# Pre-added weight blocks in DRAM: started later, of two blocks instead of three, and one more sevenfold pair in two blocks of the up-projection

## The chip, the cores and the metric

The kernel runs on one core of one Trainium2 chip. The metric is the device time of one execution in microseconds (us). The engines named here are TensorE (PE; PEld is its loading of the stationary operand), VectorE (DVE), ScalarE (ACT), GpSimd (POOL) and SyncE (SP). SP, ACT and POOL each have a queue from which they issue DMAs, in order; an instruction that waits holds up what stands behind it in its queue.

## The reference

One layer of a decoder, for 256 tokens and a width of 2048, in float32:

```
u = RMSNorm(h)
proj = u @ w_in                       # 2048 x 16896
A = HGRN2 recurrence (16 heads), B = dilated attention (3 groups of 4 heads, rotary)
h = h + (sigmoid(ga) * (A @ w_proj_a) + sigmoid(gb) * (B @ w_proj_b)) @ w_out
v = RMSNorm(h)
hup = v @ w_up                        # 2048 x 11264
a, b = causal depthwise conv (width 3) of hup, halves of 5632
h = h + (gelu(a) * b) @ w_down        # 5632 x 2048
out = RMSNorm(h)
```

## The kernel before, in words

**Weights as a stream.** All weights come as 300 units of 16 tiles of 128 x 128 (1 MB each), in the order in which TensorE uses them: units 0 to 131 are w_in, 132 to 151 the two projections of the branches, 152 to 167 w_out, and from 168 on w_up and w_down by turns. Each float32 weight is split into two parts, a rounded one (ACT, L368 or L315) and the rest (DVE, L369 or L316), and each product is made of three matmuls. `begin_unit(u)` splits units u to u + 2 and starts the load of u + 3; it also advances the side work (rotary, attention, recurrence, convolution), which stands in `side` as generators. The raw weights have three buffers, so a load waits until DVE is done with an older unit.

**Who sets the order.** The program is written for one thread; a planner then orders the instructions on each engine by their place in the program and by its own estimate of when each one's inputs and buffers are ready. `in_turn` ties a single instruction behind another. What is emitted late can therefore stand earlier on an engine, and the other way round.

**Attention at the start.** Units 0 to 35 give the queries, keys and values of the three attention groups. For each group, `rope_side` needs the halves of `aqraw` and `akraw` swapped; POOL issues two DMAs for it (L632, L633), into `xs_q` and `xs_k`, and DVE goes on at L638. POOL also issues the loads of the two masks (L676, L677) and of the level masks of the recurrence (`lev`, L737). ACT turns `lev` into `cu` (L741). `attention_side` then makes the scores, the softmax (L704, L708), transposes of the probabilities (`tr`, L715) and the output.

**The up-projection.** w_up is taken in 11 blocks of 2 x 512 columns (the a and the b half), with 8 pairs of 128 rows each. A pair is a product of two 2 x 2 block matrices. In mode "P" it is made of eight block products, in mode "S" of seven, with sums of blocks of weights and of inputs (`operands` makes the latter). A block product is three matmuls. The results go to seven sums in PSUM banks (`sevenfold`; `late_bank`), which `unfold` turns into the four wanted blocks: v = p6 - p1 comes first (L598), then ACT makes c21 and c12 from v (L603, L604), and DVE adds p7 (L605), p2 (L607), p5 (L608 and L609), p4 (L610) and p3 (L611). Blocks 0 to 2 have three "S" pairs each, blocks 3 to 10 five, together 49. `up_order` gives the order of the pairs.

**Additions in DRAM.** For each "S" pair one of the needed sums of weight blocks is made in DRAM, ahead of time: SP copies a block from DRAM to DRAM (L255), and POOL issues accumulating DMAs onto it (L256, L257), each of which waits until the one before it has landed. The load of the unit then brings three blocks of raw weights and this sum (L287, L288). `split_s` makes the other sums on DVE (L339, L340, L342). `begin_unit` spreads the additions evenly over `ADD_SPAN` units from unit `ADD_FROM` on.

**Down-projection.** Behind each block from 1 on come parts of the down-projection (`dn`), each in two banks, one for each half of the tokens; blocks 1 and 2 have two units, later blocks four, the last one more. ACT copies the result out (L1066) and POOL adds it to h by an accumulating DMA (L1067).

Of the kernel before, what the change touches and what calls it, by code (L numbers as in the profile page):

```python
# [11 lines left out]
F32 = mybir.dt.float32  # L12
# [3 lines left out]
ALU = mybir.AluOpType  # L16
AX = mybir.AxisListType

P = 128
T = 256  # L20
D = 2048
KD = D // P
# [9 lines left out]
FB = 4  # L32
# [6 lines left out]
UP_PAIRS = "SSPSSPSP"  # L39
# [11 lines left out]

def up_modes(b):

    return "PPPSSPSP" if b < 3 else UP_PAIRS


BOTH = (0, 1)
# [2 lines left out]
def up_order(b):  # L60


    return {0: (0, 1, 2, 5, 3, 7, 4, 6), 1: (0, 1, 2, 3, 5, 4, 6, 7), 2: (0, 1, 2, 3, 5, 4, 6, 7)}.get(b, tuple(range(KD // 2)))

# [63 lines left out]
NUNITS = len(stream_spec()[0]) // UNIT  # L130
MODES = stream_spec()[1]
ADDS = sum(mode == "S" for mode in MODES.values())
ADD_FROM, ADD_SPAN = 20, 140

# [49 lines left out]
def hybrid_block(ctx, tc, x_p, x_t, weights, g1, gf, params, c_rope, c_mask0, c_mask1, c_level, out):  # L186
    nc = tc.nc
    vec, act, pe = nc.vector, nc.scalar, nc.tensor
# [16 lines left out]
    def stage(name):  # L205
        return late["stage"].tile([P, 512], F32, tag="o2", name=name, bufs=6 if "pool" in late else STAGES - 2)
# [4 lines left out]
    def e4(shape, name):  # L211
        return sbe.tile([P] + list(shape), F32, tag="e4", name=name, bufs=4)
# [4 lines left out]
    def bank(i, name):  # L217
        return ps8.tile([P, 512], F32, tag=f"b{i}", name=name)

    def main_bank(name):  # L220
        turn[0] += 1
        return bank((turn[0] - 1) % 4, name)
# [20 lines left out]
    raws, splits, late = {}, {}, {}  # L243
    dram = ctx.enter_context(tc.tile_pool(name="dram", bufs=1, space=bass.MemoryType.DRAM))
    loaded, ready, to_add = [], {}, deque(sorted(u for u, mode in MODES.items() if mode == "S"))

    def add_blocks():

        if not to_add:
            return  # L250
        u = to_add.popleft()
        ready[u] = q = dram.tile([P, 512], F32, tag=f"q2_{u}", name=f"q2_{u}")
        b = [weights[u, :, i * 512 : (i + 1) * 512] for i in range(4)]
        with in_turn(loaded[-1]):
            nc.sync.dma_start(q, b[3])  # L255
        nc.gpsimd.dma_start(q, b[0], accum_op=ALU.add)  # L256
        nc.gpsimd.dma_start(q, b[2], accum_op=ALU.add)  # L257

    ring = [0]
    last = [None, None]  # L260
# [1 line left out]
    @contextmanager  # L262
    def in_turn(*instructions):

        with ExitStack() as stack:
            for i in instructions:
                stack.enter_context(tc.issue_after(i.ins))
            yield
# [44 lines left out]
    def two_parts(hi, lo, src):  # L313

        act.activation(hi, src, AF.Copy)  # L315
        vec.tensor_tensor(lo, src, hi.bitcast(F32), op=ALU.subtract)  # L316

    def pair_tile(name):

        more = late.get("pool")  # L320
        n = ring[0] % (6 if more else 4)
        ring[0] = (n + 1) if more else (n + 1) % 4
        pool, bufs = (wp, 4) if n < 4 else (more, 2)
        return pool.tile([P, 2, 1024], F32R, tag="pair", name=name, bufs=bufs)

    def split_s(u):

        r = raws[u].rearrange("p (b n) -> p b n", b=4)
        pool = late["pool"]

        def parts(name, src):
            t = pair_tile(name)
            hi, lo = t[:, 0].rearrange("p (b n) -> p b n", b=2), t[:, 1].rearrange("p (b n) -> p b n", b=2)
            two_parts(hi, lo, src)
            return [(hi[:, i], lo[:, i]) for i in range(2)]

        b11, b21 = parts(f"sa{u}", r[:, 0:2])
        b22, q2 = parts(f"se{u}", r[:, 2:4])
        vec.tensor_tensor(r[:, 0], r[:, 3], r[:, 0], op=ALU.subtract)  # L339
        vec.tensor_tensor(r[:, 1], r[:, 3], r[:, 1], op=ALU.add)  # L340
        q3, q4 = parts(f"sf{u}", r[:, 0:2])
        vec.tensor_tensor(r[:, 3], r[:, 3], r[:, 2], op=ALU.subtract)  # L342
        g = pool.tile([P, 2, 512], F32R, tag="sg", name=f"sg{u}", bufs=1)
        two_parts(g[:, 0], g[:, 1], r[:, 3])
        splits[u] = {"11": b11, "21": b21, "22": b22, "q3": q3, "q2": q2, "q4": q4, "q1": (g[:, 0], g[:, 1])}

    def split(u):
        if u >= NUNITS or u in splits:
# [36 lines left out]
    def pump(us):  # L385
        debt[0] += us
        while side and debt[0] > 0:
            try:
                debt[0] -= next(side[0])
            except StopIteration:  # L390
                side.popleft()
        if not side:
            debt[0] = min(debt[0], 0.0)

    def drain():
        while side:
            for _ in side[0]:
                pass
            side.popleft()
        debt[0] = 0.0  # L400

    def begin_unit(u):
        for v in range(u, u + LOOKAHEAD + 1):
            split(v)
        load(u + LOOKAHEAD + 1)
        pump(SIDE_US)
        if u >= ADD_FROM and (u - ADD_FROM) * ADDS // ADD_SPAN < ADDS:
            while len(to_add) > ADDS - 1 - (u - ADD_FROM) * ADDS // ADD_SPAN:
                add_blocks()
# [110 lines left out]
    def moving_step(pst, parts, k, k0, nk):  # L520

        hi, lo = next_tiles(4)
        for m in range(2):
            xh, xl = parts(k, m)
            pe.matmul(pst[m], xl, hi, start=(k == k0), stop=False)  # L525
            pe.matmul(pst[m], xh, hi, start=False, stop=False)  # L526
            pe.matmul(pst[m], xh, lo, start=False, stop=(k == k0 + nk - 1))  # L527

    def moving(parts, k0, nk, name, pst=None):

        pst = pst or [main_bank(f"{name}_{m}") for m in range(2)]
        for k in range(k0, k0 + nk):
            moving_step(pst, parts, k, k0, nk)
        return pst
# [2 lines left out]


    PRODUCTS = {
        "S": ((1, "a11", "11"), (2, "a12", "21"), (6, "x2", "q2"), (3, "x4", "22"), (7, "x3", "q3"), (4, "a22", "q4"), (5, "x1", "q1")),  # L540
        "P": (
            (2, "a11", "11"), (2, "a12", "21"), (4, "a21", "11"), (4, "a22", "21"),
            (5, "a21", "12"), (5, "a22", "22"), (3, "d1", "12"), (3, "d2", "22"),
# [32 lines left out]
    def sevenfold(ops, modes_of, order, name):  # L576

        sums = {i: late_bank(i, f"{name}_{i}") for i in range(1, 8)}
        left = {i: sum(p[0] == i for mode in modes_of for p in PRODUCTS[mode]) for i in sums}
        fresh = set(sums)  # L580
        for i in order:
            w = next_pair()
            for b, x, n in PRODUCTS[modes_of[i]]:
                (xh, xl), (wh, wl) = ops[i][x], w[n]
                left[b] -= 1
                pe.matmul(sums[b], xl, wh, start=b in fresh, stop=False)  # L586
                pe.matmul(sums[b], xh, wh, start=False, stop=False)  # L587
                pe.matmul(sums[b], xh, wl, start=False, stop=left[b] == 0)  # L588
                fresh.discard(b)
        return sums  # L590
# [269 lines left out]
    def four(name, by_half=False):  # L860

        t = e4([2, HG, P], name) if name[0] == "q" else w4([2, HG, P] if by_half else [HG, T], name)
        for h in range(HG):
            ps = stationary(x_pair, KD, f"{name}p{h}")
            if by_half:
                second = w1(f"{name}t{h}")
                act.activation(second, ps[:, T:], AF.Copy)
                vec.tensor_tensor(t[:, :, h], halves(ps[:, :T]), halves(second), op=ALU.add)
            else:
                summed(ps, t[:, h], f"{name}t{h}")  # L870
        if by_half:
            r = halves(rstd)[:, :, None, :].to_broadcast([P, 2, HG, P])
        else:
            r = rstd[:, None, :].to_broadcast([P, HG, T])
        vec.tensor_tensor(t, t, r, op=ALU.mult)
        return t
# [6 lines left out]
    for g in range(NGRP):  # L883
        z = four(f"z{g}", True)
        f = e4([2, HG, P], f"f{g}")
        act.activation(f, z, AF.Sigmoid)
        act.activation(z, z, AF.Sigmoid, scale=-1.0)
        for h in range(HG):
            i = g * HG + h
            vec.tensor_scalar(f[:, :, h], f[:, :, h], lb[:, 1, i : i + 1], lb[:, 0, i : i + 1], op0=ALU.mult, op1=ALU.add)  # L890
            vec.tensor_scalar(z[:, :, h], z[:, :, h], lb[:, 1, i : i + 1], None, op0=ALU.mult)
        q = four(f"q{g}", True)
# [4 lines left out]
        pst = moving(x_parts, 0, KD, f"gp{g}")  # L897
# [79 lines left out]
    for j in range(NJ):  # L977
        pst = moving(mix_parts, 0, KD, f"wo{j}")
# [23 lines left out]
    def late_bank(i, name):  # L1002
        return bank(place[i], name)
# [50 lines left out]
    for b in range(NBLK):  # L1054
        sums = sevenfold(hv, up_modes(b), up_order(b), f"up{b}")
        drain()
        side.append(hidden_side(b, sums))
        pump(0.0001)
        for j, b0, b1 in DOWN.get(b, ()):
            pst = moving(ff_parts, b0 * FB, (b1 - b0) * FB, f"dn{b}_{j}", [late_bank(i, f"dn{b}_{j}_{i}") for i in ((4, 5) if j % 2 else (1, 6))])  # L1060
            for m in range(2):
                if b == NBLK - 1:
                    vec.tensor_tensor(ht[j][:, m], ht[j][:, m], pst[m], op=ALU.add)
                else:
                    t = stage(f"dns{b}_{j}_{m}")
                    act.activation(t, pst[m], AF.Copy)  # L1066
                    nc.gpsimd.dma_start(ht[j][:, m], t, accum_op=ALU.add)  # L1067
# [9 lines left out]
    for m in range(2):  # L1077
# [16 lines left out]
        v, r, t = v3[:, mc], r3[:, mc], s3[:, mc]  # L1094
# [57 lines left out]
```

## Time and profile before

| | |
|---|---|
| median of three runs | 1750.25 us (1747.96 to 1752.4) |
| profiled execution | 1752.61 us, its span 1750.8 us |
| mean granted TensorE clock | 0.994 |
| ACT busy | 1035.4 us (59%) |
| POOL busy | 120.5 us (7%) |
| accumulates of POOL onto a sum (L256, L257) | 98, of 256 KB, median 6.4 us to landing |
| copies of SP (L255) | 49, of 256 KB, median 5.6 us |

How to read the lines of the profile that follow: times are us from the start of the span. A row of a timeline has start, duration, engine, line of the kernel, operation, and output <- inputs by tile names without their numbers; in brackets stands the idle time of that engine before it and what ended it. A row of the waits has the engine and what it did next, what it waited for, the sum, the number of times and the longest. A row of a table of stretches has the stretch, its length, the busy time of PE, PEld, DVE, ACT and POOL with the number of instructions, the granted clock of TensorE (1.00 is full), the busy share of the 16 DMA engines and GB/s. Matmuls overlap, so the distance of two starts, not the duration, is what one costs.

### The profile page before, as it was taken

Reading aid. Unit: us, or ns where it says so; the run is one execution under the profiler, and the core shown is the slowest. Engines: PE = TensorE matmul, PEld = TensorE weight load, DVE = VectorE, ACT = ScalarE, POOL = GpSimd, SP = SyncE. Lnnn points to the kernel's source line nnn. Section 1 sums busy time; section 2 is a strip of 40 time slices with the busy share of each in tenths; the row PEclk is TensorE's granted clock in tenths of the full one; section 3 lists DMA queues with packets and bytes.
Section 4 is the critical chain, followed back from the end, with each engine's and each line's share of the span. In section 5 each row is a group of like instructions: output and inputs, shape, how many; then the busy total and the mean of one; then the engine's idle time right before and its main releaser. Section 6 shows DMA issues by size and latency. Waiting matters only on the chain.

```text
span 1750.8 us, 21856 instructions
## 1 busy us (share of the span) xinstructions
PE 1720.1 (98%) x8325; PEld 1441.0 (82%) x8325; DVE 1299.6 (74%) x1562; ACT 1035.4 (59%) x1414; POOL 120.5 (7%) x159
## 2 busy tenths in 40 slices
PE   9999879999999999999999999999999999999998
PEld 7888768888888888888888888788888888888886
DVE  7665547586867766544565678899999989989986
ACT  6444346555555454544443667778777776776773
POOL 0001110000000010001010000000000000000000
PEclk9999989999999999999999999999999999999999
DMA  7668755767776776688887756656666566566562
GB/s 276 230 209 248 199 171 163 221 216 204 216 216 211 217 219 213 209 247 229 279 255 233 222 170 215 214 194 201 222 227 220 188 229 228 176 233 235 185 253 96
DMA packets 81785, 376.05 MB, mean 215 GB/s; under 512 B 9312, under 2 KB 9568, under 8 KB 49808
## 3 DMA queue, kind: packets, MB, share of 16 engines
q1 hardware_dynamic: 59616, 330.87, 52.7%
q0 software_dynamic: 20768, 40.38, 14.2%
q10 hardware_dynamic: 1296, 3.41, 0.5%
q8 instruction: 65, 1.06, 0.2%
q14 instruction: 40, 0.33, 0.1%
HBM read 359.94 MB, written 40.63 MB: 229 GB/s over the span
## 4 chain that ended last, share of the span: by engine, by line
PE 87%; issue 6%; DMA 4%; DVE 2%; ACT 1%; SPq 0%; POOL 0%; DVEq 0%; ACTq 0%; POOLq 0%
PE up L586 7%; PE up L588 7%; PE up L587 7%; PE dn L525 4%; PE dn L527 4%; PE dn L526 4%; PE egp L526 3%; PE egp L525 3%; PE egp L527 3%; DMA q<-weights 2%; PE aq L438 2%; PE ak L438 2%; PE gp L525 2%; PE wo L525 2%; PE gp L527 2%
## 5 line engine op out<-in xcount | busy, mean ns | idle before, releaser
L368 ACT ACTIVATE hl<-raw 128x1024 fp32r<-128x1024 f32 (+1 forms) x502 | 526.0, 1055 | 520.3 <-PE egp L527 79.4
L369 DVE TENSOR_TENSOR hl<-raw,hl 128x1024 fp32r<-128x1024 f32 (+1 forms) x502 | 605.5, 1219 | 303.9 <-ACT hl L368 301.8
L525 PE MATMUL dn<-hl,ff 128*128 128x512 f32 x320 | 127.2, 397 | 0.0
L527 PE MATMUL dn<-hl,ff 128*128 128x512 f32 x320 | 124.9, 390 | 0.0
L526 PE MATMUL dn<-hl,ff 128*128 128x512 f32 x320 | 124.7, 390 | 0.0
L525 PE MATMUL egp<-hl,xu 128*128 128x512 f32 x256 | 100.5, 393 | 0.0
L527 PE MATMUL egp<-hl,xu 128*128 128x512 f32 x256 | 99.8, 390 | 0.0
L526 PE MATMUL egp<-hl,xu 128*128 128x512 f32 x256 | 99.7, 389 | 0.0
L315 ACT ACTIVATE sf<-raw 128x1024 fp32r<-128x1024 f32 x49 | 52.3, 1067 | 69.3 <-DVE raw L340 69.0
L586 PE MATMUL up<-hl,hva 128*128 128x512 f32 x198 | 77.3, 390 | 0.0
L587 PE MATMUL up<-hl,hva 128*128 128x512 f32 x198 | 77.2, 390 | 0.0
L588 PE MATMUL up<-hl,hva 128*128 128x512 f32 x198 | 77.1, 389 | 0.0
L256 POOL DMA_DIRECT2D q<-weights x49 | 40.1, 818 | 501.4 <-DMA q<-weights 501.4
L1067 POOL DMA_DIRECT2D h<-dns x36 | 31.1, 917 | 617.8 <-ACT dns L1066 610.8
L527 PEld LDWEIGHTS dn<-hl,ff 128*128 128x128 f32 x320 | 60.1, 188 | 12.9
L525 PEld LDWEIGHTS dn<-hl,ff 128*128 128x128 f32 x320 | 60.1, 188 | 11.7
L526 PEld LDWEIGHTS dn<-hl,ff 128*128 128x128 f32 x320 | 60.2, 188 | 11.6
L438 PE MATMUL ak<-xu,hl 128*128 128x512 f32 x192 | 68.0, 399 | 0.0
L316 DVE TENSOR_TENSOR se<-raw,se 128x1024 fp32r<-128x1024 f32 x49 | 59.8, 1221 | 9.6 <-ACT se L315 9.6
L316 DVE TENSOR_TENSOR sf<-raw,sf 128x1024 fp32r<-128x1024 f32 x49 | 59.9, 1222 | 9.0 <-ACT sf L315 9.0
L316 DVE TENSOR_TENSOR sa<-raw,sa 128x1024 fp32r<-128x1024 f32 x49 | 59.8, 1221 | 4.5 <-ACT sa L315 3.7
L315 ACT ACTIVATE sa<-raw 128x1024 fp32r<-128x1024 f32 x49 | 52.0, 1062 | 14.6 <-PE up L588 6.6
(587 smaller groups left out, 4420.2 us busy)
## 6 DMA issues: line engine op xcount, KB each, us to landing
raw<-weights SPq DMA_DIRECT2D x249, 1024.0 KB, 5.3
raw<-weights SPq DMA_DIRECT2D x49, 768.0 KB, 4.3
q<-weights POOLq DMA_DIRECT2D x98, 256.0 KB, 6.4
q<-weights SPq DMA_DIRECT2D x49, 256.0 KB, 5.6
raw<-q SPq DMA_DIRECT2D x49, 256.0 KB, 4.6
h<-dns POOLq DMA_DIRECT2D x36, 256.0 KB, 3.8
h<-x_t ACTq DMA_DIRECT2D x4, 512.0 KB, 5.7
xt<-x_p SPq DMA_DIRECT2D x3, 512.0 KB, 10.0
```

The source lines that it names most:

```text
L256: nc.gpsimd.dma_start(q, b[0], accum_op=ALU.add)
L315: act.activation(hi, src, AF.Copy)
L316: vec.tensor_tensor(lo, src, hi.bitcast(F32), op=ALU.subtract)
L368: last[0] = act.activation(hi[:, q * w : (q + 1) * w], raw, AF.Copy)
L369: last[1] = vec.tensor_tensor(lo[:, q * w : (q + 1) * w], raw, hi[:, q * w : (q + 1) * w].bitcast(F32), op=ALU.subtract)
L438: pe.matmul(ps, hi, pair, start=(k == 0), stop=False, skip_group_check=True)
L525: pe.matmul(pst[m], xl, hi, start=(k == k0), stop=False)
L526: pe.matmul(pst[m], xh, hi, start=False, stop=False)
L527: pe.matmul(pst[m], xh, lo, start=False, stop=(k == k0 + nk - 1))
L586: pe.matmul(sums[b], xl, wh, start=b in fresh, stop=False)
L587: pe.matmul(sums[b], xh, wh, start=False, stop=False)
L588: pe.matmul(sums[b], xh, wl, start=False, stop=left[b] == 0)
```

## The change

Five edits. The additions begin at unit 44 and are spread over 120 units, instead of from 20 over 140. A sum in DRAM is now made of two blocks (a copy and one accumulate) (blocks 0 and 3 of the unit) and is q1; `split_s` makes q2 from it on DVE by adding block 2, in a tile of its own, and takes q3 and q4 from q2 as before. The seven products of an "S" pair are issued with product 5 third and product 6 last, instead of 6 third and 5 last. Blocks 1 and 2 of w_up have pair 0 in mode "S" too, with pair 1 issued ahead of it, so there are 51 "S" pairs. The parts of the down-projection use the banks of sums 1 and 5, and 4 and 6, in turn, instead of 1 and 6, and 4 and 5.

```diff
--- before.py
+++ after.py
@@ -51,7 +51,7 @@
 
 def up_modes(b):
 
-    return "PPPSSPSP" if b < 3 else UP_PAIRS
+    return {0: "PPPSSPSP", 1: "SPPSSPSP", 2: "SPPSSPSP"}.get(b, UP_PAIRS)
 
 
 BOTH = (0, 1)
@@ -60,7 +60,7 @@
 def up_order(b):
 
 
-    return {0: (0, 1, 2, 5, 3, 7, 4, 6), 1: (0, 1, 2, 3, 5, 4, 6, 7), 2: (0, 1, 2, 3, 5, 4, 6, 7)}.get(b, tuple(range(KD // 2)))
+    return {0: (0, 1, 2, 5, 3, 7, 4, 6), 1: (1, 0, 2, 3, 5, 4, 6, 7), 2: (1, 0, 2, 3, 5, 4, 6, 7)}.get(b, tuple(range(KD // 2)))
 
 
 
@@ -130,7 +130,7 @@
 NUNITS = len(stream_spec()[0]) // UNIT
 MODES = stream_spec()[1]
 ADDS = sum(mode == "S" for mode in MODES.values())
-ADD_FROM, ADD_SPAN = 20, 140
+ADD_FROM, ADD_SPAN = 44, 120
 
 
 
@@ -249,12 +249,11 @@
         if not to_add:
             return
         u = to_add.popleft()
-        ready[u] = q = dram.tile([P, 512], F32, tag=f"q2_{u}", name=f"q2_{u}")
+        ready[u] = q = dram.tile([P, 512], F32, tag=f"q1_{u}", name=f"q1_{u}")
         b = [weights[u, :, i * 512 : (i + 1) * 512] for i in range(4)]
         with in_turn(loaded[-1]):
             nc.sync.dma_start(q, b[3])
         nc.gpsimd.dma_start(q, b[0], accum_op=ALU.add)
-        nc.gpsimd.dma_start(q, b[2], accum_op=ALU.add)
 
     ring = [0]
     last = [None, None]
@@ -335,14 +334,15 @@
             return [(hi[:, i], lo[:, i]) for i in range(2)]
 
         b11, b21 = parts(f"sa{u}", r[:, 0:2])
-        b22, q2 = parts(f"se{u}", r[:, 2:4])
-        vec.tensor_tensor(r[:, 0], r[:, 3], r[:, 0], op=ALU.subtract)
-        vec.tensor_tensor(r[:, 1], r[:, 3], r[:, 1], op=ALU.add)
+        q2 = pool.tile([P, 512], F32, tag="q", name=f"q{u}", bufs=1)
+        vec.tensor_tensor(q2, r[:, 2], r[:, 3], op=ALU.add)
+        b22, q1 = parts(f"se{u}", r[:, 2:4])
+        vec.tensor_tensor(r[:, 0], q2, r[:, 0], op=ALU.subtract)
+        vec.tensor_tensor(r[:, 1], q2, r[:, 1], op=ALU.add)
         q3, q4 = parts(f"sf{u}", r[:, 0:2])
-        vec.tensor_tensor(r[:, 3], r[:, 3], r[:, 2], op=ALU.subtract)
         g = pool.tile([P, 2, 512], F32R, tag="sg", name=f"sg{u}", bufs=1)
-        two_parts(g[:, 0], g[:, 1], r[:, 3])
-        splits[u] = {"11": b11, "21": b21, "22": b22, "q3": q3, "q2": q2, "q4": q4, "q1": (g[:, 0], g[:, 1])}
+        two_parts(g[:, 0], g[:, 1], q2)
+        splits[u] = {"11": b11, "21": b21, "22": b22, "q3": q3, "q1": q1, "q4": q4, "q2": (g[:, 0], g[:, 1])}
 
     def split(u):
         if u >= NUNITS or u in splits:
@@ -537,7 +537,7 @@
 
 
     PRODUCTS = {
-        "S": ((1, "a11", "11"), (2, "a12", "21"), (6, "x2", "q2"), (3, "x4", "22"), (7, "x3", "q3"), (4, "a22", "q4"), (5, "x1", "q1")),
+        "S": ((1, "a11", "11"), (2, "a12", "21"), (5, "x1", "q1"), (3, "x4", "22"), (7, "x3", "q3"), (4, "a22", "q4"), (6, "x2", "q2")),
         "P": (
             (2, "a11", "11"), (2, "a12", "21"), (4, "a21", "11"), (4, "a22", "21"),
             (5, "a21", "12"), (5, "a22", "22"), (3, "d1", "12"), (3, "d2", "22"),
@@ -1057,7 +1057,7 @@
         side.append(hidden_side(b, sums))
         pump(0.0001)
         for j, b0, b1 in DOWN.get(b, ()):
-            pst = moving(ff_parts, b0 * FB, (b1 - b0) * FB, f"dn{b}_{j}", [late_bank(i, f"dn{b}_{j}_{i}") for i in ((4, 5) if j % 2 else (1, 6))])
+            pst = moving(ff_parts, b0 * FB, (b1 - b0) * FB, f"dn{b}_{j}", [late_bank(i, f"dn{b}_{j}_{i}") for i in ((4, 6) if j % 2 else (1, 5))])
             for m in range(2):
                 if b == NBLK - 1:
                     vec.tensor_tensor(ht[j][:, m], ht[j][:, m], pst[m], op=ALU.add)
```

## The prediction

> **What bounds the kernel now.** I read the page first, for the share of each engine and the granted clock by slice.
>
> ```profile
> span 1750.8 us, 21856 instructions
> PE 1720.1 (98%) x8325; PEld 1441.0 (82%) x8325; DVE 1299.6 (74%) x1562; ACT 1035.4 (59%) x1414; POOL 120.5 (7%) x159
> HBM read 359.94 MB, written 40.63 MB: 229 GB/s over the span
> ```
>
> TensorE is busy for 1720.1 of 1750.8 us. So there are two ways to gain: fewer matmuls, or less of the 30.7 us in which it idles and of the time in which it runs at a lower clock. The second question goes to the table of stretches, in steps of 50 us and then of 4 us (columns: length, PE, PEld, DVE, ACT, POOL busy, PE clock, DMA share, GB/s).
>
> ```profile
> 150.00:200.00 50.00, 48.55 (x263) 41.46 (x262) 27.94 (x29) 20.33 (x26) 6.64 (x10) 1.00 0.83 229
> 200.00:250.00 50.00, 32.47 (x152) 27.44 (x151) 18.25 (x23) 15.94 (x23) 5.61 (x8) 0.83 0.57 167
> 212.00:216.00 4.00, 4.00 (x12) 3.14 (x12) 4.00 (x4) 0.22 (x1) 0.00 (x0) 0.62 0.37 68
> 240.00:244.00 4.00, 0.60 (x4) 0.60 (x4) 2.32 (x4) 3.37 (x7) 0.00 (x0) 0.50 0.10 12
> 244.00:248.00 4.00, 4.00 (x16) 3.52 (x15) 2.27 (x5) 1.82 (x3) 0.00 (x0) 0.50 0.77 315
> 248.00:252.00 4.00, 4.00 (x25) 3.71 (x25) 2.87 (x6) 1.05 (x3) 0.87 (x1) 0.86 0.49 164
> ```
>
> Of the 30.7 us of idle time, 17.5 lie between 200 and 250 us and 1.45 in the 50 us before; most of the rest is the start and the last output. After each of two pauses the clock is low, too. The waits of TensorE name the place, and the timelines of POOL, DVE and ACT what holds it.
>
> ```profile
> PE tr L715 <- DVE sm L708: 13.0, 1, 13.0
> PE avp L527 <- DVE hl L369: 4.5, 1, 4.5
> PE ak L439 <- DVE hl L369: 1.4, 1, 1.4
> ```
>
> ```profile
> 198.57 0.81 POOL L256 DMA_DIRECT2D q<-weights  x1 [11.29 <-DMA q<-weights]
> 199.10 0.83 POOL L632 DMA_DIRECT2D xs_k<-akraw  x1
> ...
> 221.13 0.82 POOL L256 DMA_DIRECT2D q<-weights  x1 [11.65 <-DMA q<-weights]
> 221.68 0.88 POOL L676 DMA_DIRECT2D mask<-c_mask  x1
> 228.27 0.84 POOL L257 DMA_DIRECT2D q<-weights  x1 [5.72 <-DMA q<-weights]
> ...
> 229.39 0.88 POOL L737 DMA_DIRECT2D lev<-c_level  x1
> ```
>
> ```profile
> 192.59 0.42 DVE L451 TENSOR_TENSOR akraw<-ak,akt 128x256 f32<-128x256 f32 x1
> ...
> 209.19 1.23 DVE L638 TENSOR_TENSOR xs_k<-xs_k,rope 128x1024 f32<-128x1024 f32 x1 [11.07 <-DMA xs_k<-akraw]
> ```
>
> ```profile
> 236.87 3.74 ACT L741 ACTIVATE cu<-lev 128x512 uint8<-128x512 f32 x7 [12.98 <-DMA lev<-c_level]
> ```
>
> What the reader is to see: POOL's queue stands before each accumulate of an addition (11.29, 11.65, 5.72 us), until the copy or the accumulate before it has landed. Behind it in the same queue wait the half swap of the keys (xs_k), the masks and the level table (lev). The late swap stops DVE for 11.07 us, the split of the next weights waits behind it, and TensorE idles 4.5 us. The late table stops ACT for 12.98 us, the softmax behind it waits, and TensorE, at the transposes of the probabilities, idles 13.0 us. Additions, not arithmetic, cause the one large hole.
>
> **The change part by part.** The sum is made against the profiled execution, 1752.61 us (span 1750.8, and 1.8 around it); it lies 2.4 above the median of 1750.25, and I take the differences over to the median.
>
> *Additions from unit 44 on instead of 20.* From unit 20 on, one each 140 / 49 = 2.86 units, nine additions begin before unit 44: nine copies on SP and eighteen accumulates on POOL. They leave the time up to the first matmul of unit 44, the values of the first recurrent group:
>
> ```profile
> 295.85 0.58 PE L525 MATMUL vp<-hl,xu 128*128 128x512 f32 x1
> ```
>
> POOL's queue then holds, up to that point, only the six swaps, the masks and lev. How long a swap takes with no addition in front is seen in the two earlier rounds:
>
> ```profile
> 87.47 1.22 DVE L638 TENSOR_TENSOR xs_k<-xs_k,rope 128x1024 f32<-128x1024 f32 x1 [2.76 <-DMA xs_k<-akraw]
> ...
> 110.36 1.22 DVE L638 TENSOR_TENSOR xs_q<-xs_q,rope 128x1024 f32<-128x1024 f32 x1 [3.03 <-DMA xs_q<-aqraw]
> ```
>
> A DVE wait of about 3 us cost TensorE nothing there; it works two units ahead. So the idle time goes: 17.5 + 1.45 = 19.0 us. Lost to the low clock, from the rows above, busy time by (1 - clock): 4.00 x 0.38 + 0.60 x 0.50 + 4.00 x 0.50 + 4.00 x 0.14 = 4.4 us. Together 23.4. Bounds: 0, if these loads wait for something else as well, and 23.4; I take 23.4, as I find no second cause: xs_k needs only akraw, which DVE had ready at 193.0 us (it was issued at 199.1), and the masks and the table come from constants. What is late next is the table: ACT came to it at 236.87 - 12.98 = 223.9, and it landed 7.5 us after its issue. Issued right behind xs_k, at about 195, it has some 20 us in hand.
>
> The Trainium skill's TensorE: Matmul & The Clock Gate, Part 1, says that the clock halves after about 3.4 us of idling and comes back after about 3.4 us of work. By it the two pauses would cost an estimated 1.7 us each, and the sum would be 1.0 us smaller; the trace agrees in kind (0.50 after the pause of 13 us), but its second slow spell lasts longer.
>
> *Additions of two blocks, and their end.* One accumulate per addition goes: 98 become 51. Copies, loads of 768 KB and loads of the sum go from 49 to 51 each, full loads from 249 to 247. The last addition is due at unit 162, the first sevenfold unit is loaded at 169 and is the first added, so none is late. Additions come every 2.35 units instead of 2.86, but with two transfers instead of three. TensorE has no idle time in the stage that they now fill, so this brings nothing and costs nothing. Its cover is the two units of lookahead; a load that misses it would cost what it misses.
>
> *The split on DVE.* Three sums of 512 columns before (L339, L340, L342), three after; the four differences stay. The sum q2 now goes to a tile of its own, so the raw buffer is free one or two DVE steps earlier. Zero; hidden under TensorE's matmuls, and DVE's count is the same.
>
> *One pair in blocks 1 and 2 from eight products to seven.* Three matmuls per product:
>
> ```profile
> 1119.34 0.39 PE L525 MATMUL dn<-hl,ff 128*128 128x512 f32 x1
> ...
> 1120.02 0.39 PE L525 MATMUL dn<-hl,ff 128*128 128x512 f32 x1
> ```
>
> These two are three matmuls apart, 0.68 us, so one costs 0.227 (its 0.39 overlaps with the next), and 2 x 3 x 0.227 = 1.4 us go. In return DVE does per pair one large and one small difference and three small sums more. Its own spacing:
>
> ```profile
> 1157.93 0.69 DVE L316 TENSOR_TENSOR sg<-raw,sg 128x512 fp32r<-128x512 f32 x1
> 1158.53 1.22 DVE L316 TENSOR_TENSOR sa<-raw,sa 128x1024 fp32r<-128x1024 f32 x1
> 1159.67 1.22 DVE L316 TENSOR_TENSOR se<-raw,se 128x1024 fp32r<-128x1024 f32 x1
> ```
>
> A small one takes 0.60 us, a large one 1.14, so 1.14 + 4 x 0.60 = 3.5 us. Is there room?
>
> ```profile
> 1077.00:1131.00 54.00, 54.00 (x250) 44.27 (x249) 50.49 (x60) 44.21 (x69) 1.78 (x2) 1.00 0.61 204
> 1131.00:1186.20 55.20, 54.19 (x246) 44.62 (x245) 47.35 (x56) 39.94 (x59) 3.47 (x4) 1.00 0.63 205
> ```
>
> In block 1 DVE has 3.5 us left, and TensorE will be 0.7 shorter: 0.7 us too little, for once, against a lead of two units (some 10 us); block 2 has 7.8 left. I take 0; bounds 0 and 0.7.
>
> *Product order and banks.* The sums of the seven products lie in PSUM banks 1 to 7. Product 6 becomes the last of a sevenfold pair, 5 the third, and the first down-projection after a block uses banks 1 and 5 instead of 1 and 6. Bank 6 was read first when a block is unfolded; bank 5 is read last at L609. At the first and last of the ten blocks with a down-projection:
>
> ```profile
> 1122.48 0.75 DVE L609 SCALAR_TENSOR_TENSOR up1c<-up,rstd_r,up1c 128x512 f32<-128x512 f32 x1
> ...
> 1675.12 0.39 PE L525 MATMUL dn<-hl,ff 128*128 128x512 f32 x1
> ...
> 1675.83 0.74 DVE L609 SCALAR_TENSOR_TENSOR up10c<-up,rstd_r,up10c 128x512 f32<-128x512 f32 x1
> ```
>
> In program order bank 5 is wanted three matmuls (0.68 us) after the down-projection begins: at 1120.02 and 1675.80. It is free at 1123.23 and 1676.57: waits of 3.2 and 0.8 us. The ten blocks give 3.2, 1.0, 1.9, 0.8, 0.9, 0, 0.2, 0, 0.3 and 0.8, together 9.1. But the planner pulls other matmuls forward where it sees a bank late:
>
> ```profile
> 1077.90 0.40 PE L586 MATMUL up<-hl,hvs 128*128 128x512 f32 x1
> 1078.13 0.45 PE L586 MATMUL up<-hl,hvb 128*128 128x512 f32 x1
> ```
>
> The program writes L586, L587, L588 for each product; here two L586 follow each other, so one product was put into another. The down-projection's half in bank 1 has 12 to 24 matmuls (2.7 to 5.4 us) to pull forward. Bounds 0 and 9.1; I take 2, nearer to the reordered row.
>
> Block 0 ends with two sevenfold pairs and no down-projection follows. Its unfolding begins with product 6 (the first row is now its last matmul, the third that of the block):
>
> ```profile
> 1072.78 0.39 PE L588 MATMUL up<-se,hvx 128*128 128x512 f32 x1
> ...
> 1073.38 0.68 DVE L598 TENSOR_TENSOR up0v<-up,up0t 128x512 f32<-128x512 f32 x1
> ...
> 1075.50 0.39 PE L588 MATMUL up<-sg,hvx 128*128 128x512 f32 x1
> ```
>
> Product 6 will be done where the last matmul of the block now is, 1075.9 (with the 0.39) instead of 1073.2, so banks 4, 5 and 3 come free 2.7 us later, while block 1 wants them. The pairs 1 and 0 of block 1 offer 12 matmuls in banks 1 and 2 to pull forward. Bounds 0 and 2.7; I take 1.
>
> The sum: 23.4 + 1.4 - 2 - 1 = 21.8 us less. 1752.6 becomes 1730.8, and the median 1750.25 becomes 1728.5.
>
> **The rivals.** *The banks cost in full.* For it: L609 ends after the wish in eight of ten blocks, and DVE is busy for 50.49 of 54 us in block 1. Against it: the reordered rows. It takes 9.1 + 2.7 + 0.7 = 12.5 instead of 3: 1738.
>
> *The hole goes only in part*, because masks or table are held by a buffer still in use, or the swap by other loads. For it: mask and lev were issued in one go with a queue that had other reasons to be late, so a second wait would not show. Against it: swaps in the free queue landed in time twice. If the smaller stop goes and half of the 13 us stays, with its slow clock: about 9 us less gain, 1737. If nothing of it goes, the change does not do what it says: 1750.25 - 1.4 + 3 = 1752, no change.
>
> *Slower: the bank waits cost the clock.* If each of the ten waits for bank 5 leaves TensorE at half clock as after the pause of 13 us (0.30 + 2.00 + 0.56 = 2.9 us), ten waits cost 9.1 + 29 = 38 us, and 38 + 1 - 24.8 = 14 more than before: 1764. It decides from about 2.4 us for each of the ten blocks on. Against it speaks this row, where TensorE stopped for a microsecond in block 2 and the clock in that stretch stayed at 1.00:
>
> ```profile
> PE ub1t L1016 <- ACT ua1e L1024: 1.0, 1, 1.0
> ```
>
> The same page of the Trainium skill speaks for it in A second HAM failure mode: psum-queue depth-cycling: small pauses from cycling through PSUM banks can make the clock oscillate. By this rule the result would be the 1764 above; no row here shows it, and only the wait of 3.2 us in block 1 comes near the length of a pause that did lower the clock (4.5 us, 0.62).
>
> **How the numbers follow.** My forecast, 1728.5 with small costs (1723 to 1733), has a chance of 0.70; the banks in full 0.14; the hole in part 0.09; no gain 0.04; slower 0.03. The range reaches from 1722 (bank costs 0, the pause of 1.0 us gone too, and the 2 us by which runs of this kernel differ) to 1740 (banks in full, and the same 2 us). About 0.3%, 5 us, can be told from no change by the three runs shown (1747.96 to 1752.4). The first three cases are faster, 0.93; the fourth is the same, 0.04.
>
> **What would show it.** Right: the clock by slice has no dip near 240 us; TensorE is busy for about 50 of 50 us in every stretch from 50 to 1100; POOL issues masks and lev before 215 us; no wait of tr on sm above 2 us; PE x8319; POOL issues 51 accumulates; about 29 MB written (38.5 of the 40.63 MB are 49 x 3 x 0.262, now 51 x 2 x 0.262 = 26.7). Wrong: waits of dn or up on L609, L610 or L611, together above 5 us; a lowered clock after 1077; DVE at its limit in block 1 with up waiting for sa, se or sf; or lev still issued late with nothing ahead of it in the queue.

## The result, and the profile after

The changed kernel takes 1733.19 us in the median of four runs (1731.82 to 1734.15), the kernel before 1750.88 (1747.96 to 1752.4): a ratio of 0.990, 95% interval 0.9883 to 0.9917. That is 17.7 us faster; 21.8 were forecast, 1728.5 in 1722 to 1740. The time lies just above the upper end of the case that was held most likely (small costs, 1723 to 1733). A second measurement on another occasion gave 1733.19 again (1732.41 to 1733.6).

The page of the changed kernel, and then its table of stretches where the hole was (window, length, busy time of PE, PEld, DVE, ACT and POOL with counts, granted clock, DMA share, GB/s):

```profile
span 1730.5 us, 21723 instructions
PE 1715.7 (99%) x8319; PEld 1434.2 (83%) x8319; DVE 1304.3 (75%) x1572; ACT 1038.7 (60%) x1418; POOL 82.7 (5%) x112
HBM read 348.14 MB, written 28.84 MB: 218 GB/s over the span
```

```profile
150.00:200.00 50.00, 50.00 (x268) 42.81 (x267) 28.61 (x30) 21.02 (x25) 3.67 (x7) 1.00 0.65 217
200.00:250.00 50.00, 50.00 (x297) 43.66 (x296) 34.08 (x55) 31.70 (x50) 0.00 (x0) 1.00 0.45 164
```

TensorE now works through both stretches (50.00 of 50.00 us, at clock 1.00), has six matmuls less, and 28.84 MB are written (29 forecast). The timelines of POOL, DVE and ACT in the changed kernel (start, duration, engine, line, operation; in brackets the wait before it) show why:

```profile
190.04 0.51 POOL L632 DMA_DIRECT2D xs_k<-akraw  x1 [21.59 <-DVE akraw L451]
190.54 0.52 POOL L633 DMA_DIRECT2D xs_k<-akraw  x1
191.04 0.57 POOL L676 DMA_DIRECT2D mask<-c_mask  x1
191.60 0.56 POOL L677 DMA_DIRECT2D mask<-c_mask  x1
192.15 0.55 POOL L737 DMA_DIRECT2D lev<-c_level  x1
269.09 0.89 POOL L256 DMA_DIRECT2D q<-weights  x1 [76.39 <-DMA q<-weights]
...
198.09 1.23 DVE L638 TENSOR_TENSOR xs_k<-xs_k,rope 128x1024 f32<-128x1024 f32 x1 [3.17 <-DMA xs_k<-akraw]
...
214.20 3.74 ACT L741 ACTIVATE cu<-lev 128x512 uint8<-128x512 f32 x7
```

POOL issues swap, masks and table in one go once `akraw` is there; the table goes out at 192.15 instead of 229.39. DVE waits 3.17 us for the swap instead of 11.07, ACT no longer waits for the table. What TensorE waits for instead:

```profile
PE dn L525 <- DVE up6c L609: 1.3, 1, 1.3
PE warm L379 <- POOL c L235: 1.0, 1, 1.0
PE up L588 <- DVE hl L369: 0.7, 1, 0.7
PE up L588 <- DVE sf L315: 0.7, 1, 0.7
```

These are the four longest. But for the one at the start of the program (`warm`), they now lie in the up-projection: one for bank 5 (L609) in block 6, two for splits of weights in blocks 1 and 2.

By stage, between the two profiled executions, from the first matmul of w_up, of the down-projection of block 3, and of the last output:

| | before | after | difference |
|---|---|---|---|
| start to w_up | 1033.3 | 1008.3 | -25.0 |
| w_up, blocks 0 to 3 (to their down-projections) | 195.1 | 196.5 | +1.3 |
| from there to the last output | 492.2 | 494.6 | +2.5 |
| last output to the end of the span | 30.2 | 31.1 | +0.9 |

That is 20.3 us. The medians differ by 17.7, because the profiled execution before lies 1.7 above its median and the one after 0.9 below.

### The profile page after: what moved, and what is told of

Read it like the earlier page. It is cut to its first block, busy times and chain, and to the rows that moved or that the text cites. A ratio compares the mean times of both kernels' runs of the same rounds, so it can differ in the third digit from the quotient of the medians.

```text
span 1730.5 us, 21723 instructions
## 1 busy us (share of the span) xinstructions
PE 1715.7 (99%) x8319; PEld 1434.2 (83%) x8319; DVE 1304.3 (75%) x1572; ACT 1038.7 (60%) x1418; POOL 82.7 (5%) x112
## 3 DMA queue, kind: packets, MB, share of 16 engines
HBM read 348.14 MB, written 28.84 MB: 218 GB/s over the span
## 4 chain that ended last, share of the span: by engine, by line
PE 92%; DVE 4%; DMA 1%; ACT 1%; issue 1%; SPq 0%; DVEq 0%; ACTq 0%
PE up L588 7%; PE up L586 7%; PE up L587 7%; PE dn L525 4%; PE dn L527 4%; PE dn L526 4%; PE egp L526 3%; PE egp L525 3%; PE egp L527 3%; PE ak L438 3%; PE aq L438 2%; PE wo L526 2%; PE gp L525 2%; PE wo L525 2%; PE gp L527 2%; PE gp L526 2%
## 5 line engine op out<-in xcount | busy, mean ns | idle before, releaser
L369 DVE TENSOR_TENSOR hl<-raw,hl 128x1024 fp32r<-128x1024 f32 (+1 forms) x498 | 601.0, 1218 | 295.7 <-ACT hl L368 293.7
```

The lines of the kernel that those rows point to most:

```text
L369: last[1] = vec.tensor_tensor(lo[:, q * w : (q + 1) * w], raw, hi[:, q * w : (q + 1) * w].bitcast(F32), op=ALU.subtract)
```

## The experiments

All times are medians. They come from three occasions, on each of which the kernel before ran too (1750.7, 1750.8 and 1749.2 us); the first column names the occasion. The kernel before differs by up to 1.6 us between them, so differences of that size between kernels of two occasions say little by themselves.

| occasion | kernel | us | range | ratio, 95% interval |
|---|---|---|---|---|
| 1 | late additions of three blocks, nothing else | 1728.55 | 1728.20 to 1729.07 | 0.9861 to 0.9895 |
| 1 | the change, additions early | 1737.72 | 1736.13 to 1740.16 | 0.9913 to 0.9946 |
| 1 | before, masks and table from ACT's queue | 1741.85 | 1739.47 to 1744.56 | 0.9940 to 0.9971 |
| 2 | before, masks and table issued earlier | 1736.93 | 1732.33 to 1737.59 | 0.9895 to 0.9927 |
| 3 | the change, additions from unit 36 | 1733.68 | 1732.70 to 1734.48 | 0.9903 to 0.9933 |
| 1 | the change, without pairs | 1731.11 | 1729.93 to 1732.34 | 0.9875 to 0.9910 |
| 2 | late additions of three blocks, with pairs | 1728.42 | 1727.56 to 1728.92 | 0.9853 to 0.9882 |
| 2 | the change, other banks | 1729.02 | 1728.55 to 1729.70 | 0.9857 to 0.9886 |
| 3 | other banks, without pairs | 1730.70 | 1730.59 to 1731.12 | 0.9887 to 0.9917 |
| 3 | other banks, other order in block 0 | 1728.24 | 1727.35 to 1728.90 | 0.9870 to 0.9904 |
| 3 | other banks, five pairs in block 2 | 1729.59 | 1728.31 to 1729.74 | 0.9877 to 0.9911 |

**Where the gain comes from.** First only the start of the additions, in the kernel before:

```diff
-ADD_FROM, ADD_SPAN = 20, 140
+ADD_FROM, ADD_SPAN = 44, 120
```

> The kernel before with one edit, additions from unit 44 over 120 units; they stay additions of three blocks, and pairs, product order and banks stay. Theory A (the hole near 240 us comes from POOL's queue, in which swaps, masks and table stand behind additions): the whole 23 us go, 1727 to 1729 against 1750.9, that is some 5 us below the changed kernel, which pays for banks and pairs. Theory B (the second accumulate of each addition is what costs): half or less of it, 1740 or more.

Measured: 1728.55, as theory A says. One line of the change is worth 22.1 us, more than the whole change; all that is left of it costs 4.6. Its table of stretches shows no hole either:

```profile
200.00:250.00 50.00, 50.00 (x296) 43.65 (x295) 34.15 (x54) 31.30 (x49) 0.00 (x0) 1.00 0.47 169
```

Then the other way round, all of the change but this line:

```diff
-ADD_FROM, ADD_SPAN = 44, 120
+ADD_FROM, ADD_SPAN = 20, 140
```

> The changed kernel with its additions put back to unit 20 over 140 units; they are of two blocks. Theory A: most of the hole stays, since the waits for the copy stay in POOL's queue and only those before the second accumulate (5 to 8 us each) are gone: the table comes about 7 us earlier, so the pause of 13 us shrinks to about 6, and the time is 1738 to 1744. Theory B: no hole, 1733, like the changed kernel.

Measured: 1737.72, just below what theory A gave. So one accumulate less does shrink the hole by itself, but does not remove it. It shrinks it by more than was expected: the table went out at 207.56, 22 us earlier and not 7, since every accumulate that is gone from POOL's queue brings forward all that stands behind it. In the waits of TensorE of this kernel, and its finer table around the second pause:

```profile
PE tr L715 <- DVE sm L708: 2.8, 1, 2.8
```

```profile
226.00:228.00 2.00, 1.83 (x7) 1.71 (x8) 1.94 (x4) 0.63 (x2) 0.00 (x0) 0.58 0.89 116
228.00:230.00 2.00, 2.00 (x9) 1.69 (x8) 0.67 (x3) 0.77 (x1) 0.00 (x0) 0.57 0.93 320
230.00:232.00 2.00, 2.00 (x18) 1.92 (x17) 1.68 (x2) 0.56 (x2) 0.00 (x0) 1.00 0.47 197
```

The pause of 13.0 us has become one of 2.8, and the clock still drops to 0.58 behind it.

**Queue or traffic.** Two kernels leave the additions of the kernel before alone and take only masks and table from behind them. First, to ACT's queue, `mask0` and in the same way `mask1` and `lev`:

```diff
-    nc.gpsimd.dma_start(mask0, c_mask0)
+    act.dma_start(mask0, c_mask0)
...
```

> The kernel before with one edit: the loads of the two masks and of the level table are issued from ACT's queue instead of POOL's; the additions stay where and as they were, with all their traffic. Theory A: the pause of 13 us and its slow clock (2.9 us) go, the pause of 4.5 us behind the swap of the keys stays: 1735. Theory C (the traffic of the additions on the DMA engines and in memory makes these loads late, whatever their queue): no change, 1751.

Measured: 1741.85, between the two. The timeline of ACT in this kernel tells why:

```profile
217.67 0.54 ACTq L737 DMA_DIRECT2D lev<-c_level  x1
228.73 3.75 ACT L741 ACTIVATE cu<-lev 128x512 uint8<-128x512 f32 x7 [6.11 <-DMA lev<-c_level]
```

ACT's queue is in order, too, and stands behind splits that the late swap of the keys holds up; so the table went out at 217.67, only 12 us earlier. Then it took 11.0 us to land instead of 7.4, while the DMA engines were full (DMA share 0.94 to 1.03 between 216 and 228 us): weight loads go out again once TensorE has restarted. That is not due to ACT's queue: in the kernel with early additions of two blocks the table took 12.0 us from POOL's queue, at a share of 0.95 to 1.01. So traffic adds to the wait, and this run could not separate the two. The second kernel writes the same loads, still on POOL's queue, ahead of the loop over the second and third attention group; their old places are empty:

```diff
+    mask0, mask1 = w4([AG, P], "mask0"), w4([AG, T], "mask1")
+    nc.gpsimd.dma_start(mask0, c_mask0)
+    nc.gpsimd.dma_start(mask1, c_mask1)
...
+    nc.gpsimd.dma_start(lev, c_level[:, : NL * P].rearrange("p (l m t) -> p l m t", l=NL, m=2))
     for j in range(1, AG):
```

> The kernel before with the loads of masks and level table written ahead of the second attention group, still on POOL's queue; the additions stay where and as they were, with all their traffic. Theory A (what stands behind additions in POOL's queue is late): no wait for the table, so the pause of 13 us and its slow clock go, and the pause behind the swap of the keys (4.5 us and 1.5 of clock) stays: 1735. Theory C (traffic, not the queue): the pause stays in some other place, 1742 or more, as with the loads on ACT's queue.

Measured: 1736.93; the profiled execution is its fastest, 1732.33. The table went out at 59.6 us, ahead of all additions. TensorE's waits:

```profile
PE ub1t L1017 <- ACT ua1e L1025: 2.2, 1, 2.2
PE avp L527 <- DVE hl L369: 1.5, 1, 1.5
```

With every addition and all its bytes in place, there is no wait for tr on sm any more; the pause of 13 us is gone. The swap of the keys still stands behind an addition (DVE waits 8.05 us for it). The three other executions took 1736.86 to 1737.59, with a mean clock of 0.997 instead of 0.999; no trace shows what held them.

This edit takes the loads out of the time of the additions as well as from behind them in the queue, so by itself it does not exclude traffic. The landing times of the table do. They are, in the kernel before, in the changed one, and in the one with early additions of two blocks:

```profile
DMA to landing us min/median/max: 7.4/7.4/7.4
```

```profile
DMA to landing us min/median/max: 8.9/8.9/8.9
```

```profile
DMA to landing us min/median/max: 12.0/12.0/12.0
```

With additions beside it, the table landed no later after its issue in the kernel before than without them in the changed one. What differs is the issue, 229.39 against 192.15. For the table it was the place in the queue. For the swap of the keys it was so for the larger part: from `akraw` being ready to the first issue it took 6.1 us before and 0.3 after, from there to the landing 10.1 and 8.0.

How early may additions start? Unit 36 is the first behind the masks and the table in the program:

```diff
-ADD_FROM, ADD_SPAN = 44, 120
+ADD_FROM, ADD_SPAN = 36, 128
```

> The changed kernel with additions from unit 36 over 128 units, which is right behind the masks and the table in the program and about 45 us earlier than unit 44. Theory A (only what stands behind them in POOL's queue matters): the same as the changed kernel, 1733.2 within 1 us, though the attention at 220 to 300 us now has the traffic of additions beside it. Theory C (traffic): 1735 or more.

Measured: 1733.68, the same, with two accumulates between 200 and 250 us (DMA share 0.57 instead of 0.45). The traffic of additions beside the attention costs nothing that shows.

**What the rest costs.** Without the additional pairs, and with the order of products in blocks 1 and 2 that goes with it:

```diff
-    return {0: "PPPSSPSP", 1: "SPPSSPSP", 2: "SPPSSPSP"}.get(b, UP_PAIRS)
+    return "PPPSSPSP" if b < 3 else UP_PAIRS
...
-    return {0: (0, 1, 2, 5, 3, 7, 4, 6), 1: (1, 0, 2, 3, 5, 4, 6, 7), 2: (1, 0, 2, 3, 5, 4, 6, 7)}.get(b, tuple(range(KD // 2)))
+    return {0: (0, 1, 2, 5, 3, 7, 4, 6), 1: (0, 1, 2, 3, 5, 4, 6, 7), 2: (0, 1, 2, 3, 5, 4, 6, 7)}.get(b, tuple(range(KD // 2)))
```

> The changed kernel without the additional sevenfold pairs (blocks 1 and 2 as before, 49 pairs). If the pairs bring their six matmuls and cost nothing: 1.4 us slower than the changed kernel, 1734.6. If DVE in blocks 1 and 2 gives back the 1.1 us that the traces show lost there: the same within 0.5 us, 1733.

Measured: 1731.11, and not 1734.6. The pairs make the changed kernel some 2 us slower (the ranges of the two kernels overlap by 0.5 us), though they save six matmuls. Both expectations missed. The traces show most of it in two places. In block 2 a load of weights comes late on ACT, ahead of the split for which TensorE then waits (0.3 and 0.7 us); this wait is not there without the pairs. And in block 6, far behind the pairs, ACT waits 2.82 us for a load with the pairs (the row is shown below) and 1.29 without, and TensorE's wait of 1.3 us for bank 5 is not there without. First ACT in block 2 of the changed kernel, then in block 6 without the pairs:

```profile
1140.69 1.06 ACT L368 ACTIVATE hl<-raw 128x1024 fp32r<-128x1024 f32 x1 [1.86 <-DMA raw<-weights]
```

```profile
1390.22 2.01 ACT L368 ACTIVATE hl<-raw 128x1024 fp32r<-128x1024 f32 x2 [1.29 <-DMA raw<-weights]
```

Why loads come later with the pairs stays open. Are the pairs too much for DVE, or do they cost only with the new banks? With late additions of three blocks, the split and order of products and the banks of the kernel before, and `up_modes` and `up_order` of the change (the lines marked - in the last diff):

> The kernel before with late additions of three blocks and with the additional pairs; product order, banks and split stay as before. Theory D (the pairs cost because DVE cannot keep up in blocks 1 and 2): 0.5 to 2 us slower than late additions alone (1728.55). Theory E (they cost only together with the new product order and banks): the six matmuls' 1.4 us show, 1727.2.

Measured: 1728.42 against 1728.55 without pairs, between the two theories. Blocks 0 to 3 became 0.5 us shorter instead of 1.4 (194.8 against 195.3), as there is a new wait:

```profile
PE up L586 <- DVE up0c L605: 1.6, 1, 1.6
```

This is bank 7 of block 0, at the start of block 1. So the pairs give back about what they save, but not more. The banks then, with the pairs of the change:

```diff
-            pst = moving(ff_parts, b0 * FB, (b1 - b0) * FB, f"dn{b}_{j}", [late_bank(i, f"dn{b}_{j}_{i}") for i in ((4, 6) if j % 2 else (1, 5))])
+            pst = moving(ff_parts, b0 * FB, (b1 - b0) * FB, f"dn{b}_{j}", [late_bank(i, f"dn{b}_{j}_{i}") for i in ((4, 7) if j % 2 else (1, 6))])
```

> The changed kernel with one edit: the parts of the down-projection take banks 1 and 6, and 4 and 7, in turn, so that the first one after a block does not need bank 5, which is read last. If the waits for L609 (1.45 us in block 6, 0.1 in each other block) cost what the trace shows: 2 us less than the changed kernel, 1731. If they only cover a wait for late weights: the same within 0.7 us.

Measured: 1729.02, against 1733.19 of the changed kernel on the same occasion: 4.2 us less, twice of what was expected. For comparison both kernels from the down-projection of block 3 on, the changed one first:

```profile
1204.75:1699.36 494.61, 493.32 (x2232) 406.39 (x2231) 446.14 (x514) 364.45 (x532) 25.67 (x30) 1.00 0.63 214
```

```profile
1203.65:1695.76 492.11, 492.11 (x2231) 406.95 (x2230) 445.68 (x515) 364.11 (x531) 25.67 (x30) 1.00 0.63 215
```

TensorE has no idle time left with the other banks. The second row begins one matmul (0.23 us) later in the program than the first; from the same matmul on, the stretch is 2.3 us shorter. Block 6 shows how bank 5 comes to cost, first in the changed kernel (ACT, DVE, TensorE), then with the other banks (ACT, DVE):

```profile
1393.63 1.06 ACT L368 ACTIVATE hl<-raw 128x1024 fp32r<-128x1024 f32 x1 [2.82 <-DMA raw<-weights]
...
1399.65 0.74 DVE L609 SCALAR_TENSOR_TENSOR up6c<-up,rstd_r,up6c 128x512 f32<-128x512 f32 x1
...
1400.45 0.50 PE L525 MATMUL dn<-hl,ff 128*128 128x512 f32 x1 [1.29 <-DVE up6c L609]
```

```profile
1391.74 2.01 ACT L368 ACTIVATE hl<-raw 128x1024 fp32r<-128x1024 f32 x2 [2.47 <-DMA raw<-weights]
...
1397.75 0.74 DVE L609 SCALAR_TENSOR_TENSOR up6c<-up,rstd_r,up6c 128x512 f32<-128x512 f32 x1
```

In both, a load of weights comes late there (2.82 and 2.47 us). It delays the split, and the unfolding behind it on ACT and DVE, to L609. With bank 5 the down-projection waits for this end of the chain; with bank 6, read first, nobody does. As much again, 2.4 us, lies in blocks 0 to 3 (196.5 against 194.1), where the two waits for splits in block 2 (0.7 and 0.3 us) are gone together with the late load before them. Why that load is in time with the other banks stays open.

The pairs again, with these banks: both edits, the banks and the taking out of the pairs, at once.

> The changed kernel with banks 1 and 6, and 4 and 7, for the down-projection and without the additional pairs. If the pairs bring their 1.4 us once the banks are out of the way: 1730.4, against 1729.0 with them. If they are worth nothing there, too, as in the old order: 1729.0. Against late additions of three blocks alone (1728.55) it has only the new order of products and the additions of two blocks left.

Measured: 1730.70 without, 1729.02 with pairs, the latter on another occasion. In the two profiles blocks 0 to 3 take 196.4 and 194.1 us, so the gain lies where the pairs are. Here the pairs make the kernel 1.7 us faster, with the banks of the change 2.1 us slower; the banks of another stage decide. Without pairs the new order of products and the additions of two blocks cost 2.1 us against late additions of three blocks alone (1730.70 against 1728.55, again on two occasions). TensorE's longest wait in that kernel is at the start of block 1:

```profile
PE up L586 <- ACT sg L314: 1.4, 1, 1.4
```

The last term was product 6 at the end of block 0, tried with the other banks:

```diff
-    return {0: (0, 1, 2, 5, 3, 7, 4, 6), 1: (1, 0, 2, 3, 5, 4, 6, 7), 2: (1, 0, 2, 3, 5, 4, 6, 7)}.get(b, tuple(range(KD // 2)))
+    return {0: (0, 1, 2, 3, 5, 4, 6, 7), 1: (1, 0, 2, 3, 5, 4, 6, 7), 2: (1, 0, 2, 3, 5, 4, 6, 7)}.get(b, tuple(range(KD // 2)))
```

> The changed kernel with banks 1 and 6, and 4 and 7, and with the pairs of block 0 in the order 0, 1, 2, 3, 5, 4, 6, 7, so that the block ends with an eightfold pair and product 6 is done 24 matmuls before its end. If the wait at the start of block 1 (0.87 us, put down to a split of weights) comes from product 6 being the last: 1 us less than 1729.0. If DVE's load in block 0 and 1 sets it: the same, or more by a few tenths, since three sevenfold pairs then come closer together.

Measured: 1728.24, 0.8 less, on another occasion; the ranges overlap, so the medians alone don't show a gain. In the profile blocks 0 to 3 take 193.4 us instead of 194.1, and the wait for the split at the start of block 1 (0.7 us, hl L369) is gone from the list:

```profile
PE avp L527 <- DVE hl L369: 0.5, 1, 0.5
PE rstd_ps L469 <- DVE ssq L486: 0.5, 1, 0.5
PE up L586 <- DVE up0c L605: 0.2, 1, 0.2
```

And one pair more in block 2, which then is like the later blocks, with the other banks as well:

```diff
-    return {0: "PPPSSPSP", 1: "SPPSSPSP", 2: "SPPSSPSP"}.get(b, UP_PAIRS)
+    return {0: "PPPSSPSP", 1: "SPPSSPSP", 2: "SSPSSPSP"}.get(b, UP_PAIRS)
...
-    return {0: (0, 1, 2, 5, 3, 7, 4, 6), 1: (1, 0, 2, 3, 5, 4, 6, 7), 2: (1, 0, 2, 3, 5, 4, 6, 7)}.get(b, tuple(range(KD // 2)))
+    return {0: (0, 1, 2, 5, 3, 7, 4, 6), 1: (1, 0, 2, 3, 5, 4, 6, 7)}.get(b, tuple(range(KD // 2)))
```

> The changed kernel with banks 1 and 6, and 4 and 7, and with five sevenfold pairs in block 2 instead of four, in natural order, as in the later blocks. Three matmuls less: 0.7 us below 1729.0 if DVE keeps up; the same or up to 1 us more if DVE, with 3.5 us more work in a block that has little room, holds TensorE.

Measured: 1729.59 (1728.31 to 1729.74), not to be told from 1729.02. One more pair shows no gain there.

The changed kernel once more, as a measure for the kernels of the second occasion:

> The changed kernel once more, on the same chip as the three beside it: 1733.2 within 1.5 us.

Measured: 1733.19.

The lowest three, 1728.24, 1728.42 and 1728.55, can't be told apart; each is some 5 us below the changed kernel. The simplest of them is the kernel before with one line changed.

## Why the prediction was right, and where its terms were off

- **The hole, -23.4.** Right in cause, place and size: -25.0 up to w_up between the two profiles, -22.1 as a median with this line alone. Behind the swap POOL issued the table at 192, against "about 195".
- **No second cause.** Right: with the table issued early and all additions in place its pause was gone, and the table did not land faster without additions (8.9 us) than with them (7.4). The rival "the hole goes only in part" fell.
- **Two blocks instead of three: nothing.** Not contradicted where the change puts the additions, but no run has it alone. At the old place the kernel with it takes 1737.72, some 13 us less than the kernel before with all the other costs in it, since half of the accumulates are gone from POOL's queue. The prediction did not price that.
- **Pairs, -1.4, DVE at most 0.7.** This is the step that failed. The six matmuls went (x8319), but the pairs made the changed kernel 2.1 us slower, so they cost some 3.5 us where 0.7 was the bound. The sum looked at DVE's load over blocks 1 and 2 alone. What showed instead was a load of weights that comes late ahead of a split in block 2, and a later load in block 6, behind which TensorE waits for bank 5. The two units of lookahead, taken as cover, were not enough there. With the old order and banks, or with banks 1 and 6, and 4 and 7, these two waits did not show.
- **Banks, 2 of 0 to 9.1.** Mis-sized: 4.2 with the pairs, nothing that can be told without (1731.11 against 1730.70, ranges that overlap). The ten waits were read from DVE's times before, where block 1 gave 3.2 us and block 6 none. It came out the other way: in block 1 the planner put six matmuls of block 2 into the down-projection and only some 0.3 us are lost; in block 6 a late load moved the unfolding, and TensorE stopped for 1.3 us. Reordering covered the wait that the planner could foresee, not the load that was late on the chip.
- **Product 6 at the end of block 0, 1 of 0 to 2.7.** Right as far as the traces show: 0.7 us in blocks 0 to 3, tried with the other banks; the medians can't tell it from nothing.
- **Sum.** Costs of pairs, order and banks: +1.6 forecast, +4.6 measured (1733.19 against 1728.55). Nearly all of the rest of the difference to 21.8 is the hole, 22.1 instead of 23.4. That the result lies in the range rests on the hole, which was read rightly; the costs together came out nearly three times as large as forecast.
- **Slower, by bank waits that cost the clock.** The longest wait for bank 5 was 1.3 us, and the clock stayed at 1.00 behind it. The rule of the Trainium skill's TensorE: Matmul & The Clock Gate, A second HAM failure mode: psum-queue depth-cycling, did not show here.

## What to carry to other kernels

A DMA queue that is in order and waits for landings is a resource like an engine: ask for each load in it what stands ahead, and when that will be done. Before work is moved or added to a queue, look for the small loads behind it on which a softmax or a mask hangs. A buffer or bank that is asked for should be the one that is freed first in the chain of its reader: here the planner's order hid a late reader, but not a late load ahead of it.

## What the runs showed of the hardware that was not expected

In one profile, that of early additions of two blocks, TensorE's clock fell behind a pause of 2.8 us (0.58 and 0.57 over the next 4 us), while pauses of 1.3, 1.6 and 2.2 us in the profiles of other kernels left it at 1.00. The Trainium skill's TensorE: Matmul & The Clock Gate, Part 1, has about 3.4 us of idling for this; the measured pause was shorter, so the measurement decides.

A load of 448 KB (the table) took 7.4 us to land from POOL's queue in the kernel before. Beside the weight loads that follow a pause, at a DMA share near 1.0, it took 11.0 us from ACT's queue and 12.0 us from POOL's. So a load that goes out late can meet the weight loads that the pause held back, and come later still.
